# Two attention loops: TensorE's order written out by hand, with top-k and index scores rearranged

## The chip, the core and the metric
The kernel runs on one core of a Trainium2 chip. Its time is the device time of one execution in microseconds; several runs are taken and their median counts. One further execution was profiled by the hardware profiler. TensorE (PE in the profile; its weight loads are PEld), VectorE (DVE), ScalarE (ACT) and GpSimd (POOL) each run their own instructions in order and wait for one another by semaphores; SyncE's queue (SP) issues DMAs.

## The reference
Two blocks, one behind the other, on 512 tokens of width 1024; the change touches the second block, in which 16 meta tokens stand ahead of the tokens (528 positions). It has a differential attention (DA, 8 heads of two scores each), a feed-forward part, a sparse attention (DSA, 16 heads in 8 pairs) and a second feed-forward part. Cut to the core:

```python
# DA: two softmaxes a head, one subtracted from the other
s = einsum('bqhcd,bkhcd->bhcqk', q, k); p = softmax(where(causal, s, -inf))
o = einsum('bhqk,bkhe->bqhe', p[:, :, 0] - lam * p[:, :, 1], v)      # then rms norm per head, @ w_o
# DSA: an index decides which 128 keys a query sees (the 16 meta tokens always)
raw = einsum('bqhd,bkd->bqhk', qi, ki) * IDX_DIM ** -0.5             # 8 index heads, one index key
score = einsum('bqhk,bqh->bqk', relu(raw), wi)
score = where(causal & (k_pos < N_META), BIG_SCORE, score)
top_val, top_idx = top_k(where(causal, score, -inf), 128)
p = softmax(scores of the chosen keys); o = p @ v                    # @ w_o
```

## The kernel before
Everything is kept transposed: features on the 128 partitions, tokens along the free dimension. A float32 matrix product is made of three products: weights and inputs are split into a high part (written by ScalarE) and a low remainder (written by VectorE), and high x high, low x high and high x low are summed in one PSUM bank. A weight chunk of 128 x 1024 (512 KB) is loaded by SP into one of four buffers (`wload`), and split by `wchunk` into `wH` (L318, ScalarE) and `wL` (L320, VectorE), of which there are four each; `wget` keeps one chunk ahead. A projection of one head (`project`) is `gemm` (L349) on one chunk: two column cuts (272 and 256 columns), 24 products each (8 blocks of 128 rows times 3), then `rope` (L821): ScalarE copies the bank, VectorE shuffles, multiplies and adds, POOL multiplies (L827 to L831).

PSUM has eight banks, given out by tag: `g` 3 (projections), `s` 2 (scores), `t` 2 (transposes), `o` 1 (the output of a head). Scores read stacked copies of q and k: `stack` (L1034) writes high part and remainder of each half of the partitions (ScalarE and VectorE, four operations each for q and k), `swapped` (L1045) copies the halves crosswise with two DMAs (`k3`). These copies have one buffer, so the next head's are written behind the last scores of this one.

A head (DA) or pair (DSA) goes over four query blocks i of 128 with growing key ranges (144, 272, 400, 528). For each: S_i makes scores, masks them (L1227 in DA, L1422 in DSA, VectorE, with the row maximum), exponentials on ScalarE (L1234, L1429), and a scaling on VectorE (L1239 subtracts the second softmax, L1435 divides). T_i is one function: `turns_of` (L1139) transposes by TensorE (L1147) and copies the banks out (L1149 VectorE, L1151 ScalarE), and the value products (L1248, L1443 and L1448) follow. N finishes the head, X writes the stacked copies for the next head. F projects k of the next head, G projects q of the one after; in DA heads 0 and 2 G first makes a quarter of the values (`project_v`, L849). In the last heads F and G are early output products (`out_first`). The meta tokens' own attention (`metas`, with L1126 and L1135) runs in head 6, one step behind each of its steps. `attend` (L1353) calls these in the order of

```python
ORDER = "S1 S2 T1 F S3 T2 S4 X T3 T4 N G".split()
```

but this sets only priorities: a planner (the tile scheduler) puts every engine's instructions in order when the program is built, by dependencies, by priority and by the times it expects. So single products of F and G stand on TensorE between the attention steps, wherever the planner expected a hole. Only `front` (L493) fixes TensorE's order by `manual_schedule`.

DSA begins with `dsa_index` (L1483): the index key `ki` with its stacked forms `k2` and `k3` (made by three ScalarE and two VectorE operations, L1516 to L1522), and for each of four index head pairs a projection over 512 columns, `rope`, `stack` (`q2`, one buffer), and scores, relu on ScalarE (L1535) and a weighted sum into `sel` on VectorE (L1539, L1541). Then come the values (four quarters of five token tiles), then `dsa_topk` (L1543): 14 rounds over the four query blocks of a maximum of eight (L1557) and their replacement (L1558) on VectorE, and then q and k of pair 0 and q of pair 1.

Of the kernel before, what the change touches and what calls it, by code (L numbers as in the profile page):

```python
# [16 lines left out]
P = 128  # L17
D = 1024
KB = 8
# [14 lines left out]
ORDER = "S1 S2 T1 F S3 T2 S4 X T3 T4 N G".split()  # L34
# [178 lines left out]
class _Kernel:  # L213
# [135 lines left out]
    def gemm(self, w, H, L, cuts, M=P, spread=False, late=False):  # L349
# [4 lines left out]
        for c0, cn in cuts:  # L354
# [11 lines left out]
            yield ps[:M, :cn], c0, cn  # L366

# [771 lines left out]
    def turns_of(self, pool, srcs, name, width):  # L1139

        nc = self.nc
        t = pool.tile([P, width * P], F32, name=name)
        for c0 in range(0, len(srcs), 4):
            ps = self.ps("t")
            n = min(4, len(srcs) - c0)
            for j in range(n):
                nc.tensor.transpose(ps[:, P * j:P * j + P], srcs[c0 + j], self.ident)  # L1147
            if c0 == 4:
                nc.vector.tensor_copy(t[:, P * c0:P * (c0 + n)], ps[:, :P * n])  # L1149
            else:  # L1150
                nc.scalar.activation(t[:, P * c0:P * (c0 + n)], ps[:, :P * n], AF.Copy)  # L1151
        return [t[:, P * j:P * j + P] for j in range(len(srcs))]
# [10 lines left out]
    def da(self, g_next):  # L1163
        nc, T = self.nc, T2
        with ExitStack() as ctx:
# [38 lines left out]
            qk, scores, ps_, sums = {}, {}, {}, {}  # L1204

            def project(h, nm):

                t = self.acc if nm == "q" else self.rb
                self.rope(wp, self.gemm(self.wblocks(KB), self.hH, self.hL, self.cuts(T)), C, S, t)
                self.meta_keep(h, nm, t)  # L1210
                qk[nm] = t
# [4 lines left out]
            def soft(h, i):  # L1216

                t0, e = STARTS[i], ENDS[i]
                mx = self.sm.tile([P, 4], F32, name="mx2")
                p = ps_[i] = wp.tile([P, 2, T2], F32, name="p")  # L1220
                den = self.sm.tile([P, 4], F32, name="den2")
                m = 1 if i < 4 else 2
                for r in range(2):
                    for u, (pp, k0, k1) in enumerate(scores[h](i, r)):
# [4 lines left out]
                                                       accum_out=mx[:, c:c + 1])  # L1229
                if m == 2:  # L1230
                    nc.vector.tensor_tensor(mx[:, 0:2], mx[:, 0:4:2], mx[:, 1:4:2], ALU.max)
# [8 lines left out]

            def apply(h, i, po):

                a = ps_[i][:, 0]

                aT = self.turns_of(wp, [a[:, :P]] + [a[:, META + P * j:META + P * j + P] for j in range(i)], "aT", 5)
# [47 lines left out]
            def start(h, i, po):  # L1293
# [4 lines left out]
                soft(h, i)  # L1298
# [15 lines left out]
            def fill(h, op):  # L1314
                if op == "F":
                    if h < 7:
                        project(h + 1, "k")
                    else:
                        self.out_first(OH, OL, (2, 3, 4))
                else:  # L1320
                    if h in (0, 2):
                        self.project_v(vs, 2 + h // 2, self.vweights(), self.tok_tiles(T))
                    if h < 6:
                        project(h + 2, "q")
                    else:
                        self.out_first(OH, OL, (0, 1) if h == 6 else (5, 6, 7))

            project(0, "q")
            project(0, "k")
            stacks(0)  # L1330
            project(1, "q")
            self.attend({"S": start, "T": apply_flip, "N": finish, "X": stacks}, fill, metas)
# [5 lines left out]
    def out_first(self, H, L, ms, lo=0):  # L1338

        for m in ms:  # L1340
            for ps, c0, cn in self.gemm(self.wblocks(4), H[:4], L[:4], self.cuts(T2, lo)):
                x = self.x[m][:, c0:c0 + cn]
                self.nc.vector.tensor_tensor(x, ps, x, ALU.add)

# [8 lines left out]
    def attend(self, fns, fill, meta):  # L1353


        for h in range(8):
            po = self.ps("o")
            for op in ORDER:
                if op in ("F", "G"):
                    fill(h, op)  # L1360
                    if h == 6 and op == "F":
                        meta = meta()
                elif op == "X":
                    if h < 7:
                        fns["X"](h + 1)
                elif op[0] == "N":
                    fns["N"](h, po)
                else:
                    fns[op[0]](h, int(op[1]), po)
                    if h == 6 and not callable(meta):  # L1370
                        next(meta, None)

    def dsa(self, g_next):
# [3 lines left out]
        with ExitStack() as ctx:  # L1377
# [8 lines left out]
            with ExitStack() as ictx:  # L1386
                self.dsa_index(self.pool(ictx, "ei", 1, reuse_waits="tile"), C, S, sel)
                for q in range(4):
                    self.project_v(vs, q, self.vweights(), self.tok_tiles(T), meta=v0)
                self.dsa_topk(sel)  # L1390
# [5 lines left out]
            qk, scores, ps = {}, {}, {}  # L1396
# [5 lines left out]
            def project(b, nm):  # L1402
                t = self.acc if nm == "q" else self.rb
                cuts = self.cuts(T, lo if nm == "q" else 0)
                self.rope(wp, self.gemm(self.wblocks(KB), self.hH, self.hL, cuts), C, S, t)
                self.meta_keep(b, nm, t, lo)
                qk[nm] = t
# [4 lines left out]
            def soft(b, i, po):  # L1412
# [3 lines left out]
                mx = self.sm.tile([P, 4], F32, name="mx2")  # L1416
# [262 lines left out]
```

## Time and profile before

| | us |
|---|---|
| median of 3 runs (2151.54 to 2156.41) | 2152.59 |
| profiled execution | 2149.52 |
| its span, from the first to the last instruction | 2147.5 |

| busy in the span | PE | PEld | DVE | ACT | POOL |
|---|---|---|---|---|---|
| us | 2064.2 | 1885.1 | 1487.0 | 1023.3 | 277.8 |
| share | 96% | 88% | 69% | 48% | 13% |

The first block takes about the first 700 us, DA 700 to 996, the feed-forward part to 1393, DSA to about 1750 (index, values and top-k to 1527), the last feed-forward part the rest. Matmuls overlap in the pipeline and their ends are modelled, so a PE that is busy need not be at its peak; an instruction's duration is its way through the pipeline and not its distance to the next. Idle time of an engine is put down to what ended it. Window rows give busy time with the number of instructions; PEclk is the granted share of TensorE's clock.

### The profile page before, as it was taken

The numbers are of one execution on the slowest core, as the hardware profiler recorded it, in microseconds if no ns is written. First come the engines' busy times: TensorE is split into PE (matmuls) and PEld (weight loads), VectorE is DVE, ScalarE is ACT, GpSimd is POOL, SyncE is SP. The second block draws the span as 40 slices with busy tenths as digits, with TensorE's granted clock in tenths as the row PEclk, the third lists the DMA queues.
The fourth block names the chain that finished last, engine by engine and source line by source line (L and its number), as shares of the span: only waits on it lengthen the run. The fifth ranks groups of instructions, "written<-read, shape, count | busy, mean of one in ns | idle before, by whom it ended". The sixth has DMA issues, their size and how long they took to land.

```text
span 2147.5 us, 37629 instructions
## 1 busy us (share of the span) xinstructions
PE 2064.2 (96%) x14812; PEld 1885.1 (88%) x14812; DVE 1487.0 (69%) x3215; ACT 1023.3 (48%) x1874; POOL 277.8 (13%) x433
## 2 busy tenths in 40 slices
PE   8999999989998999889999999989899999999998
PEld 6788888877778888889999999979888899999997
DVE  7786777787776676866763566489888657735653
ACT  6876555346675455544442343353455444423431
POOL 0211111141103321212000000210211020000001
PEclk9999999999999999989999999999999999999998
DMA  5433342403212222212333333311322123332321
GB/s 192 123 117 115 96 125 94 143 25 108 68 60 70 80 72 68 71 50 80 92 95 90 90 89 89 99 50 50 100 60 76 55 73 95 89 99 89 99 81 48
DMA packets 59567, 186.11 MB, mean 87 GB/s; under 512 B 8384, under 2 KB 12480, under 8 KB 59392
## 3 DMA queue, kind: packets, MB, share of 16 engines
q1 hardware_dynamic: 58240, 182.68, 28.3%
q8 instruction: 116, 1.90, 0.4%
q10 hardware_dynamic: 1152, 1.05, 0.1%
q14 instruction: 59, 0.48, 0.1%
HBM read 171.77 MB, written 2.23 MB: 81 GB/s over the span
## 4 chain that ended last, share of the span: by engine, by line
PE 77%; DVE 11%; ACT 6%; issue 3%; POOL 1%; DMA 1%; SPq 0%; POOLq 0%; DVEq 0%; ACTq 0%
PE ps_g L364 48%; PE ps_s L364 14%; DVE wL L320 2%; PE ps_s L1062 2%; PE ps_o L1448 1%; PE ps_t L1147 1%; PE ps_g L849 1%; DVE sel L1558 1%; PE ps_o L1248 1%; DVE m L1557 1%; PE ps_s L766 1%; ACT wH L318 1%; PE ps_o L1001 1%; ACT q L1041 1%; PE ps_g L502 1%
## 5 line engine op out<-in xcount | busy, mean ns | idle before, releaser
L364 PE MATMUL ps_g<-hH,wL 128*128 128x256 f32 (+3 forms) x1856 | 590.4, 318 | 2.1 <-DVE wL L320 2.0
L364 PE MATMUL ps_g<-hH,wH 128*128 128x256 f32 (+3 forms) x1856 | 590.6, 318 | 0.0
L364 PE MATMUL ps_g<-hL,wH 128*128 128x256 f32 (+3 forms) x1856 | 590.3, 318 | 0.0
L318 ACT ACTIVATE wH<-raw 128x1024 fp32r<-128x1024 f32 x294 | 309.4, 1057 | 380.9 <-PE ps_g L364 203.3
L320 DVE TENSOR_TENSOR wL<-raw,wH 128x1024 fp32r<-128x1024 f32 x294 | 362.8, 1237 | 154.4 <-ACT wH L318 153.8
L364 PEld LDWEIGHTS ps_g<-hH,wL 128*128 128x128 f32 x1856 | 350.6, 189 | 26.0 <-DVE wL L320 3.5
L364 PEld LDWEIGHTS ps_g<-hL,wH 128*128 128x128 f32 x1856 | 350.4, 189 | 23.0 <-issue 2.9
L364 PEld LDWEIGHTS ps_g<-hH,wH 128*128 128x128 f32 x1856 | 350.4, 189 | 22.7 <-issue 1.0
L364 PE MATMUL ps_s<-hH,wH 128*128 128x256 f32 (+5 forms) x568 | 165.1, 291 | 6.6 <-ACT hH L393 6.6
L364 PE MATMUL ps_s<-hH,wL 128*128 128x256 f32 (+5 forms) x568 | 164.7, 290 | 0.0
L364 PE MATMUL ps_s<-hL,wH 128*128 128x256 f32 (+5 forms) x568 | 164.7, 290 | 0.0
L384 POOL TENSOR_TENSOR acc<-acc,sq 128x512 f32<-128x512 f32 (+3 forms) x62 | 78.7, 1269 | 545.1 <-ACT sq L383 543.8
L1600 DVE SCALAR_TENSOR_TENSOR c<-u,prm,c 128x528 f32<-128x528 f32 (+1 forms) x176 | 132.4, 755 | 1.5
L830 POOL TENSOR_TENSOR rt<-rt,S 128x272 f32<-128x272 f32 (+3 forms) x80 | 81.8, 1024 | 354.1 <-DVE rt L828 284.4
L364 PE MATMUL ps_g<-aH,wH 128*128 128x256 f32 (+1 forms) x418 | 118.7, 284 | 0.3 <-ACT aH L865 0.2
L364 PE MATMUL ps_g<-aL,wH 128*128 128x256 f32 (+1 forms) x418 | 118.7, 284 | 0.0
L364 PE MATMUL ps_g<-aH,wL 128*128 128x256 f32 (+1 forms) x418 | 118.6, 284 | 0.0
L364 PEld LDWEIGHTS ps_s<-hH,wH 128*128 128x128 f32 (+2 forms) x568 | 106.1, 187 | 8.3 <-ACT hH L393 6.6
L364 PEld LDWEIGHTS ps_s<-hH,wL 128*128 128x128 f32 (+2 forms) x568 | 106.3, 187 | 2.5 <-issue 1.0
L364 PEld LDWEIGHTS ps_s<-hL,wH 128*128 128x128 f32 (+2 forms) x568 | 106.1, 187 | 2.4 <-DVE hL L398 1.3
L1062 PE MATMUL ps_s<-k,q 128*128 128x272 f32 (+3 forms) x400 | 90.5, 321 | 12.9 <-DVE q L1042 4.3
L865 ACT ACTIVATE aH<-sg 128x528 fp32r<-128x528 f32 (+1 forms) x44 | 28.1, 639 | 124.3 <-DVE sg L1605 124.3
(551 smaller groups left out, 4586.1 us busy)
## 6 DMA issues: line engine op xcount, KB each, us to landing
raw<-in_ws_dram SPq DMA_DIRECT2D x294, 512.0 KB, 3.6
k<-k SPq DMA_DIRECT2D x32, 264.0 KB, 3.1
m<-acs_d SPq DMA_DIRECT2D x32, 256.0 KB, 3.5
e<-eas_d SPq DMA_DIRECT2D x32, 96.0 KB, 2.7
x<-in_xT_dram SPq DMA_DIRECT2D x8, 256.0 KB, 5.0
xo<-in_xT_dram SPq DMA_DIRECT2D x8, 256.0 KB, 5.6
k<-k SPq DMA_DIRECT2D x4, 256.0 KB, 6.5
out_dram<-x SPq DMA_DIRECT2D x8, 128.0 KB, 1.7
```

What stands on the lines that cost most here:

```text
L318: nc.scalar.activation(H, self.raw, AF.Copy)
L320: nc.vector.tensor_tensor(L, self.raw, H.bitcast(F32), ALU.subtract)
L364: nc.tensor.matmul(ps[:M, :cn], w[k][a][:, :M], b[k][:, c0:c0 + cn], start=i == 0, stop=i == 3 * n - 1)
L384: (eng or nc.gpsimd).tensor_tensor(acc, acc, s[:, :cn], ALU.add)
L502: mm(ps, w, h, start=k == 0 and a == 0, stop=False)
L766: nc.tensor.matmul(yd[64 * r:64 * r + 64, P * c:P * c + P], xdt[:, c, 2 * i + r, :], ms[2 * i + r][:, P * c:P * c + P], start=True, stop=True)
L830: nc.gpsimd.tensor_tensor(t, t, S[:, cc], ALU.mult)
L849: nc.tensor.matmul(ps[:tn, :256], a[k][:, t0:t0 + tn], w[k][b], start=n == 0, stop=n == 3 * KB - 1)
L865: nc.scalar.activation(H[:, cols], src, AF.Copy)
L1001: nc.tensor.matmul(po[64 * r:64 * r + 64, P * j:P * j + w], vs[j][:, 64 * kv:64 * kv + 64], pT[r][:, 256 * j:256 * j + w], start=j == 0, s ...
L1062: nc.tensor.matmul(ps, q[:, r, t0:e], k[:, r, k0:k1], start=n == 0, stop=n == 1)
L1600: nc.vector.scalar_tensor_tensor(c[:, lo:], u[:, t + lo:t + T2], self.col(fw, 3 * b + t), c[:, lo:], ALU.mult, ALU.add)
```

## The change
TensorE's order in both loops is now as written: `attend` runs inside `manual_schedule` for TensorE, with a longer ORDER. In it f and g stand for portions of F and G: a projection is four portions of 12 products (two for each cut, `portions`), and what F or G has is dealt evenly over the f's or g's that are left. T is now the transposes alone (up to two banks of four), U a third bank, V the value products, Z4 the second score of block 4 (S4 is the first). M runs a step of the meta tokens' attention, now M4 and M5 of head 6 and M1 to M3 of head 7. The early output products become half jobs of one cut (12 products): in head 6 four in G, in head 7 four in F and eight in G, the second cuts ahead of the first, and each pair of output blocks keeps its weights between. Other engines' order is still the planner's.

In DSA, `dsa_index` makes q of two index pairs ahead (two buffers for `q2`), puts two quarters of the values ahead of the scores of pairs 2 and 3, and swaps k2 into k3 by two DMAs. `dsa_topk` goes block by block; the first block, of 128 keys, looks for the 16 lowest on the negated and mirrored scores (2 rounds) in place of the 112 highest (14 rounds).

```diff
-ORDER = "S1 S2 T1 F S3 T2 S4 X T3 T4 N G".split()
+ORDER = "S1 f S2 M1 f T1 M2 S3 V1 f M3 T2 S4 V2 f Z4 T3 X g V3 M4 g g T4 g U4 V4 M5 N".split()
...
+    def portions(self, w, H, L, c0, cn, then, n=2):
...
+        def part(i):
+            if not ps:
+                ps.append(self.ps("g")[:, :cn])
+            ww = w()
+            steps = [(k, a, b) for k in range(len(H)) for a, b in ((0, H), (1, H), (0, L))]
+            m = len(steps)
+            for j in range(m * i // n, m * (i + 1) // n):
+                k, a, b = steps[j]
+                self.nc.tensor.matmul(ps[0], ww[k][a], b[k][:, c0:c0 + cn], start=j == 0, stop=j == m - 1)
+            if i == n - 1:
+                then(ps[0])
+        return [lambda i=i: part(i) for i in range(n)]
...
+        cs = list(range(0, len(srcs), 4))
+        banks(cs[:2])
+        return [t[:, P * j:P * j + P] for j in range(len(srcs))], lambda: banks(cs[2:])
...
+    def out_fill(self, H, L, h, op, lo=0):
+        if h == 6:
+            jobs = [(m, 1) for m in range(4)]
+        elif op == "F":
+            jobs = [(m, 1) for m in range(4, 8)]
+        else:
+            jobs = [(m, 0) for m in range(8)]
+        return [lambda j=j: self.out_first(H, L, [j], lo) for j in jobs]
...
+        with self.tc.manual_schedule(engines={mybir.EngineType.PE}):
+            for h in range(8):
+                po = self.ps("o")
+                todo = {op: fill(h, op.upper()) for op in "fg"}
+                for n, op in enumerate(ORDER):
+                    i = int(op[1]) if len(op) > 1 else 0
+                    if op in todo:
+                        left = ORDER[n:].count(op)
+                        for f in range(-(-len(todo[op]) // left)):
+                            todo[op].pop(0)()
+                    elif op[0] == "M":
+                        if (h, i) in ((6, 4), (6, 5), (7, 1), (7, 2), (7, 3)):
+                            next(meta, None)
...
+            self.dsa_topk(wp, sel)
+            for f in project(0, "q") + project(0, "k"):
+                f()
             stacks(0)
+            for f in project(1, "q"):
+                f()
...
-        nc.scalar.activation(k3[64:], ki[64:], AF.Copy)
-        nc.vector.tensor_tensor(k3[:64], ki[64:], k3[64:].bitcast(F32), ALU.subtract)
+        k3 = self.swapped(ip, k2, "k3")
...
+            q2[b] = self.stack(ip, q, "q2", META, 2)
...
+        project(0)
+        project(1)
+        for b in range(4):
+            if b < 2:
+                scores(b)
+                project(b + 2)
+            else:
+                values(b - 2)
+                scores(b)
+        values(2)
+        values(3)
...
-        for rnd in range((TOPK - META) // 8):
-            for i in range(1, 5):
-                m8 = self.sm.tile([P, 8], F32, name=f"m8{i}")
-                rest = sel[i][:, META:]
+            rest = neg if i == 1 else sel[i][:, META:]
+            if i == 1:
+                nc.vector.tensor_scalar(neg[:, ::-1], diag, -1.0, None, ALU.mult)
+            for rnd in range(2 if i == 1 else (TOPK - META) // 8):
+                m8 = self.sm.tile([P, 8], F32, name="m8")
                 nc.vector.max(m8, rest)
                 nc.vector.match_replace(rest, m8, rest, MARK)
```

## Rows read from the trace of the kernel before

**Rows 1.** Busy time by stretch, one row each: start and end, length, engines.
```profile
core 0: us, PE busy (x) PEld busy (x) DVE busy (x) ACT busy (x) POOL busy (x), PEclk, DMA share, GB/s
867.00:890.70 23.70, 21.09 (x162) 19.73 (x162) 19.92 (x70) 14.36 (x41) 6.04 (x12) 1.00 0.25 70
1573.10:1597.00 23.90, 23.53 (x190) 20.83 (x190) 20.37 (x67) 13.54 (x33) 4.00 (x7) 1.00 0.25 68
985.00:1392.00 407.00, 406.71 (x3336) 405.67 (x3334) 238.30 (x354) 150.45 (x184) 25.61 (x65) 1.00 0.31 91
914.50:971.80 57.30, 51.35 (x375) 48.28 (x376) 37.44 (x135) 25.64 (x76) 7.70 (x13) 0.88 0.17 48
1668.60:1725.10 56.50, 52.69 (x410) 46.46 (x411) 37.36 (x137) 24.66 (x66) 1.96 (x3) 0.94 0.17 48
1505.00:1527.30 22.30, 17.25 (x126) 16.48 (x124) 17.54 (x36) 8.32 (x14) 10.37 (x16) 0.92 0.48 143
```

**Rows 2.** Groups of TensorE's instructions in one DA head: busy, mean ns, idle before.
```profile
L1248 PE MATMUL ps_o<-v,aT 128*128 128x128 f32 x28 | 4.2, 290 | 0.6 <-ACT aT L1151 0.5
L1147 PE MATMUL ps_t<-ident,p 128*128 128x128 f32 x14 | 2.2, 276 | 2.0 <-DVE p L1239 2.0
```

**Rows 3.** Chain of work in the feed-forward stage: start, us, what.
```profile
1016.85 3.02 PE ps_g L364 x24
1019.88 2.83 PE ps_s L364 x24
```

**Rows 4.** Timeline of a DA head from S1 to T1: start, us, instruction, idle.
```profile
884.84 0.43 PE L1062 MATMUL ps_s<-k,q 128*128 128x144 f32 x2
...
886.35 0.30 DVE L1227 CUSTOM_DVE_ANT_0 p<-ps_s,wide 128x144 f32<-128x144 f32 x1
...
886.80 1.22 DVE L320 TENSOR_TENSOR wL<-raw,wH 128x1024 fp32r<-128x1024 f32 x1
...
890.97 0.41 PE L1147 MATMUL ps_t<-ident,p 128*128 128x128 f32 x2 [1.15 <-DVE p L1239]
```

**Rows 5.** The page's DMA issues, the swapped copy: count, size, us to landing.
```profile
k<-k SPq DMA_DIRECT2D x32, 264.0 KB, 3.1
```

**Rows 6.** Timeline of TensorE in DA's head 6, products of the meta tokens.
```profile
926.67 1.48 PE L1135 MATMUL ps_t<-mv,v 128*128 128x16 f32 x8 [1.82 <-DVE mv L1264]
```

**Rows 7.** Timeline of TensorE, first scores of head 0, in DA and DSA.
```profile
742.08 0.43 PE L1062 MATMUL ps_s<-k,q 128*128 128x144 f32 x2
...
746.73 0.45 PE L1062 MATMUL ps_s<-k,q 128*128 128x144 f32 x2 [1.03 <-DMA k<-k]
...
1520.74 0.33 PE L1062 MATMUL ps_s<-k,q 128*128 128x144 f32 x1 [2.86 <-DVE k L1042]
...
1527.34 0.42 PE L1062 MATMUL ps_s<-k,q 128*128 128x144 f32 x2 [0.92 <-DMA k<-k]
```

**Rows 8.** Timeline of TensorE in a DSA head: value products, then projection products.
```profile
1577.73 0.44 PE L1448 MATMUL ps_o<-pT,v 128*64 128x128 f32 x4
1578.10 0.38 PE L364 MATMUL ps_g<-hH,wL 128*128 128x256 f32 x1
1578.32 0.28 PE L364 MATMUL ps_g<-hL,wH 128*128 128x256 f32 x1
```

**Rows 9.** Top-k on VectorE: the chain, then the timeline of blocks 1 and 2.
```profile
1477.79 1.19 DVE sel L1558 x2
...
1481.20 1.19 DVE sel L1558 x2
...
1497.10 0.61 DVE L1557 MAX8 m<-sel 128x8 f32<-128x128 f32 x2
...
1497.69 0.27 DVE L1558 MATCH_REPLACE8 sel<-m,sel 128x128 f32<-128x128 f32 x1
```

**Rows 10.** Timeline of TensorE in the index: first scores of pairs 0 and 1.
```profile
1417.50 0.45 PE L1062 MATMUL ps_s<-k,q 128*128 128x144 f32 x2 [2.35 <-DVE q L1042]
...
1427.17 0.45 PE L1062 MATMUL ps_s<-k,q 128*128 128x144 f32 x2 [0.93 <-DVE q L1042]
```

More of the change, by code (lines that the diff above doesn't have):

```diff
@@ L1229, in soft @@
                                                        accum_out=mx[:, c:c + 1])
+                if 1 not in rs:
+                    return
                 if m == 2:
@@ L1336, in da, with out_first @@
             self.out_last(OH, OL, g_next)
-    def out_first(self, H, L, ms, lo=0):
-        for m in ms:
-            for ps, c0, cn in self.gemm(self.wblocks(4), H[:4], L[:4], self.cuts(T2, lo)):
+    def out_first(self, H, L, jobs, lo=0):
+        for m, half in jobs:
+            if m not in self.wo:
+                self.wo[m] = self.wblocks(4)
+            for ps, c0, cn in self.gemm(self.wo[m], H[:4], L[:4], self.cuts(T2, lo, half)):
                 x = self.x[m][:, c0:c0 + cn]
                 self.nc.vector.tensor_tensor(x, ps, x, ALU.add)
+    def out_fill(self, H, L, h, op, lo=0):
[6 more added lines that the diff above has]
+        return [lambda j=j: self.out_first(H, L, [j], lo) for j in jobs]
     def out_last(self, H, L, g_next, lo=0):
@@ L1353, in attend @@
     def attend(self, fns, fill, meta):
[L1356 to L1371, printed above, removed]
+        self.wo = {}
+        with self.tc.manual_schedule(engines={mybir.EngineType.PE}):
[11 more added lines that the diff above has]
+                            next(meta, None)
+                    elif op == "X":
+                        if h < 7:
+                            fns["X"](h + 1)
+                    elif op == "N":
+                        fns["N"](h, po)
+                    elif op[0] in "SZ":
+                        fns["S"](h, i, (0, 1) if i < 4 else (0,) if op[0] == "S" else (1,))
+                    elif op[0] == "V":
+                        fns["V"](h, i, po)
+                    else:
+                        fns[op[0]](h, i)
     def dsa(self, g_next):
@@ L1386, in dsa @@
             with ExitStack() as ictx:
[L1387 to L1390, printed above, removed]
+                values = lambda q: self.project_v(vs, q, self.vweights(), self.tok_tiles(T), meta=v0)
+                self.dsa_index(self.pool(ictx, "ei", 1, reuse_waits="tile"), C, S, sel, values)
             oc = self.pool(ctx, "eo", 1, reuse_waits="tile")
```

183 lines of the change are left out of this document (104 added, 79 removed).

## The prediction
> **What bounds the kernel now.** I read the busy times by stretch first. In the feed-forward stage TensorE is full: weight loads busy 405.67 of 407.00 us, matmuls back to back. In one steady head of the first attention (DA) weight loads are busy 19.73 of 23.70 us, VectorE 19.92; in one of the sparse attention (DSA) 20.83 of 23.90, VectorE 20.37 [rows 1]. So both loops have gaps on TensorE, and VectorE stands close behind: whatever closes the gaps, a head can't go much under 20 us. Next the groups of TensorE instructions of the DA head, for who ended the gaps: 2.0 us are transposes that wait for the softmax (DVE p), 0.6 us value products that wait for the copied transposes [rows 2]. Then the chain, for the price of dense work: 24 products of 272 columns take 3.02 us, of 256 columns 2.83 [rows 3]; so a portion of 12 is 1.51 or 1.42 us. The timelines come last, for single waits.
>
> **DA, a steady head.** Removed: the order in which the scheduler strews projection products between attention steps. A head has six such waits (2.6 us of idle), and each also shows the tail of a product, 0.28 long where the next could start after 0.12, so 6 x 0.16 = 1.0: 3.6 us in all. Added: fixed places, where every later TensorE instruction stands behind a late one. The first transposes (T1) stand behind a portion, S2 and a portion: 1.5 + 0.5 + 1.5 = 3.5 us after S1. In the trace S1 ends at 885.27 and T1 starts at 890.97, 5.7 us later, because VectorE first finished a rope and did a weight split of 1.22 us between links of the chain [rows 4]. VectorE's order is still the scheduler's, so this wait lies between 0 and 2.2 us; I take 1.0, nearer to the middle since of the 5.7 us the split (1.22) and the queue before the first score operation (1.08) are not the chain's own. T4 stands 5.9 us behind the last scores, with eight stacking operations of ScalarE and VectorE for the next head between: 0 to 1.5, I take 0.5. T2, T3 and the four value steps: 0.7 (now 0.6 by rows 2). Step X (stacks, then two DMAs of 3.1 us [rows 5] for the swapped copy) starts behind Z4 as now behind S4, for it needs the buffers; it has 9.4 us of TensorE work until the next S1 and needs about four splits and a DMA: 0.3. New waits 2.5, old 3.6: -1.1 us a head; ends -3.3 (only the value steps wait) and +2.4 (6.0 of waits). Four heads without value projections: -4.4. Heads 0 and 2 have 14 us more TensorE work (5 token tiles of 24 products) and the same softmax, so VectorE has room and its waits go: -2.5 each, -5.0. DVE, ScalarE, POOL and DMA operations stay the same in number; weight loads follow their portions, in the same order on SP's queue, and a load of 512 KB is four buffers ahead.
>
> **DA, both ends.** In head 6 no projection is left: of the last two heads' 57.30 us weight loads are busy 48.28, at a granted clock of 0.88 [rows 1], and the products of the meta tokens alone waited 1.82 us for VectorE [rows 6]. The change cuts the early output projections into 16 half jobs (1.42 to 1.51 us) and lays 4 of them and the meta steps between the steps of head 6. Its 28.4 us should come to 23.5: -4.9; head 7, with work for 27.4 in its 28.9: -1.5. All four weight chunks of the half jobs now stay in the four buffers until the second halves ran, so the next stage's first split can start only behind two of the eight jobs in head 7; six jobs (8.5 us) cover its 2.3 us, and it would cost those 2.3 if they didn't. At the start S1 of head 0 waits for the DMA of the swapped keys; now 25 products ran in that hole (742.3 to 746.7) and TensorE idled only 1.03 us [rows 7]. Fixed, they come behind S1: 25 x 0.12 = +3.0. DA in all: -4.4 - 5.0 - 4.9 - 1.5 + 3.0 = **-12.8** (ends -28 and +6).
>
> **DSA, the loop.** Idle is small, but the strewn order costs at each change of kind: a projection product behind four value products has its successor 0.22 us later [rows 8] instead of 0.12; with the way in I put an estimated 0.25 on one block. The head's timeline has twelve such blocks of transposes or value products among projections (one is shown), the new order nine: -0.75; waits for copied transposes are 0.3 idle with tails 0.75. Of these 1.5 I leave 0.5 for new waits: -1.0 us a head, six heads -6.0; ends -1.5 and +2.4 as in DA. Splitting S4 by head (S4, Z4) costs nothing: its four score products need the same two banks now, and a portion between lets VectorE empty them. U4 needs a bank that ScalarE empties in one copy, under the portion g. Heads 6 and 7 took 56.50 us at a clock of 0.94 [rows 1]; two heads at 22.9, 5.8 of extra output products and 1.5 of meta steps are 53.1: -3.4. Sum **-9.4** (ends -16 and +14).
> Weighed against a rule: the DSA head shows matmuls busy 23.53 of 23.90 us but weight loads 20.83 [rows 1]. The Trainium skill (Perfetto Trace Analysis, Identifying the Most-Contended Engine) holds matmul busy share a poor measure of headroom and weight-load share a good one. By the first the loop has 0.4 us a head to give, by the second 3.1, so six heads would give 2 or 19 instead of 6; the feed-forward row, with 405.67 of 407.00, agrees with the second, but the blocks that stay keep their price, and I stay with 1.0.
>
> **DSA, the front.** Top-k is 14 rounds of four query blocks at 3.41 us [rows 9], VectorE full all along. The first block now takes 2 rounds on the flipped sign (112 of up to 128 keys: the same choice by its complement). Its part of a round is half of the two maxima and their overlap, 0.22, and 0.25 of replacing [rows 9]: 12 x 0.47 = 5.6, less 0.4 for the two flips: -5.2. Order by block instead of by round makes each operation wait for the one before: where nothing else fills, 84 operations lose the overlap of about 0.08, +6.7; where blocks 3 and 4 or the ropes fill, 0. I take 0 as the scheduler already pairs blocks here. k3 by two DMAs in place of two ScalarE and one VectorE operation: -0.7 on VectorE; the DMA (3.1) lands while S1 still waits for q2. These waits are 2.35 us for the first q2 and 0.93 for the second, which had to wait for the only buffer [rows 10]: a second buffer takes -1.5 with the tails; the values placed between change nothing, they fill there now. After top-k 22.30 us pass until the swapped keys are there, VectorE busy 17.54 [rows 1, 7]: weight splits and ropes that stood behind top-k. In the dependent gaps of the last block some can go earlier; 0 to 8 us, I take 4. And S1 waits for the keys without filler: 26 products ran in that hole [rows 7], +3.1. The sum is -5.2 - 0.7 - 1.5 - 4.0 + 3.1 = **-8.3** (ends -15 and +4).
>
> **Sum.** -12.8 - 9.4 - 8.3 = -30.5 us against the profiled execution's 2149.52, so 2119.0; the median of the runs stands 3.07 above it: **2122**.
>
> **Rivals.** (a) *Other engines set the period*: softmax, ropes and stacks on VectorE (19.9 to 20.4 us a head and in order) hold the steady heads where they are; then only the front, the ends and the heads with values pay: -8.3 - 4.9 - 1.5 + 3.0 - 3.4 and -2 for values, -17: 2135. For it: VectorE's 84% in steady heads; against it: it idles 3.8 us there, waiting for TensorE in turn.
> (b) *The fixed order stalls*: a late softmax holds TensorE's whole queue, projections too, that now run in its place. Price: T1's full 2.2 us, T4's 1.5 and the rest 2.3, 6.0 a head; minus 3.6 it is +2.4 in DA and, with 1.5 saved less, +2.4 at most in DSA. Over 12 steady heads +29, with the ends and the front -15: 2167, slower. It decides from the point where the new waits pass 4.9 us a head in DA (3.6 + 15/12). For it: the 5.7 us of rows 4; against it: the own chain of T1 is some 3 us.
> (c) *TensorE goes dense*: hardly a new wait; DA -28, DSA loop -12, front -13: 2100.
> (d) *Top-k in order by block loses what its shorter first block gives*: the front gives 0, the rest stays: 2130.
> That the loops don't do what the change says, I can rule out: the order is written out.
>
> **How the numbers follow.** Forecast with (d) beside it 0.55, (a) 0.2, (c) 0.15, (b) 0.1. About 0.2% (4.3 us) is what a measurement of this kernel can tell from no change. Faster by more: all but (b) and a tail of (a) that comes down to nothing, 0.83; within: that tail, 0.07; slower: 0.10. The range from 2098, the ends of (c), to 2150, the tail of (a), leaves out most of (b) and what is under (c).
>
> **What would show it.** Right: steady heads of 22 to 23 us in both loops, with transposes idle under 2 us a head; head 6 of DA under 25 us at full clock; S1 of DSA's head 0 some 8 us earlier behind the index; in the loops runs of 12 products between steps. Wrong: T1 or T4 idle over 2 us a head, S1 waiting for the swapped keys in steady heads, or top-k as long as before. The biggest doubt is VectorE's order, which the change leaves to the scheduler and the trace of before can't show.

## The result, and the profile after

The changed kernel is slower: 2185.73 us median (2184.26 to 2189.62) against 2153.73 us for the kernel before on the same chip, a ratio of 1.0152 [1.0137, 1.0167]. The forecast was 2122 us and the range ended at 2150; rival (b), the fixed order that stalls, had been given 0.10 and 2167. The profiled execution of after is the one of 2189.62 us, 40 us above that of before. To find these 40 us I cut both traces at four marks: the first scores of DA, the first product of the feed-forward stage behind it, VectorE's first instruction on DSA's index keys, and DSA's first scores. The loops of all runs below are read by the same cuts; a loop here ends with the first product of the next feed-forward stage.

| us between marks | DA loop | DSA front | DSA loop |
|---|---|---|---|
| before | 254.4 | 125.3 | 232.0 |
| after | 275.0 | 129.2 | 246.1 |
| forecast | 241.6 | 117.0 | 222.6 |

All three stages went the other way; the other stages differ by 2 us together. The busy times by stretch answer rows 1 (same columns): a steady DA head, a steady DSA head, then the last head of each loop, of the changed kernel.

```profile
core 0: us, PE busy (x) PEld busy (x) DVE busy (x) ACT busy (x) POOL busy (x), PEclk, DMA share, GB/s
...
881.30:908.40 27.10, 21.11 (x164) 19.60 (x163) 21.06 (x70) 14.35 (x40) 6.09 (x12) 1.00 0.22 59
1608.60:1634.50 25.90, 22.60 (x191) 20.23 (x190) 20.45 (x67) 13.29 (x33) 3.82 (x8) 1.00 0.22 63
...
961.40:995.10 33.70, 32.75 (x239) 32.04 (x238) 21.90 (x78) 14.56 (x42) 2.70 (x6) 0.90 0.19 55
1737.30:1770.40 33.10, 31.50 (x256) 29.59 (x256) 21.02 (x74) 12.84 (x35) 0.00 (x0) 0.95 0.19 57
```

A DA head takes 27.10 us where it took 23.70, a DSA head 25.90 where it took 23.90. TensorE is not busier (weight loads 19.60 against 19.73), nor is any other engine near full: both sides wait for each other. TensorE's groups in that DA head answer rows 2:

```profile
L1082 PE MATMUL ps_s<-k,q 128*128 128x272 f32 (+3 forms) x21 | 4.6, 321 | 1.6 <-DVE mx L1266 1.3 <-DMA k<-k 0.2
L1294 PE MATMUL ps_o<-v,aT 128*128 128x128 f32 x28 | 4.0, 282 | 2.6 <-ACT aT L1173 2.6
L1169 PE MATMUL ps_t<-ident,p 128*128 128x128 f32 x14 | 2.2, 276 | 1.8 <-DVE p L1280 1.8
```

Idle is now 1.6 + 2.6 + 1.8 = 6.0 us against 2.6: the 3.4 us by which the head grew. The transposes wait about as long as before (1.8 against 2.0); new are the value products, which wait 2.6 for ScalarE's copy of the transposes, and the scores, 1.6. What ScalarE does meanwhile is in its timeline (start, us, instruction, idle before):

```profile
888.19 0.63 ACT L1275 ACTIVATE p<-p,mx 128x400 f32<-128x400 f32 x1 [1.56 <-DVE mx L1273]
888.72 0.19 ACT L1275 ACTIVATION_READ_ACCUMULATOR p<-p,mx 128x1 f32 x1
888.82 0.61 ACT L1275 ACTIVATE p<-p,mx 128x400 f32<-128x400 f32 x1
...
889.43 0.47 ACT L1173 ACTIVATE aT<-ps_t 128x384 f32<-128x384 f32 x1
```

and in TensorE's:

```profile
887.39 0.49 PE L1169 MATMUL ps_t<-ident,p 128*128 128x128 f32 x3
887.64 0.79 PE L1082 MATMUL ps_s<-k,q 128*128 128x272 f32 x4
889.95 0.94 PE L1294 MATMUL ps_o<-v,aT 128*128 128x128 f32 x6 [1.52 <-ACT aT L1173]
```

The transposes of T2 are done near 887.9, yet their copy starts at 889.43: ScalarE works in order, and the exponentials of block 3 stand ahead of the copy and themselves waited 1.56 us for VectorE. Between T2 and V2 the order has only S4 (0.8 us) as cover. In the kernel before, with scores and transposes next to each other, the same copy ran ahead of those exponentials:

```profile
872.84 0.48 ACT L1151 ACTIVATE aT<-ps_t 128x384 f32<-128x384 f32 x1
...
874.20 0.63 ACT L1234 ACTIVATE p<-p,mx 128x400 f32<-128x400 f32 x1 [0.31 <-DVE mx L1232]
```

The late end of the head shows VectorE's order, ahead of T4:

```profile
894.94 1.21 DVE L322 TENSOR_TENSOR wL<-raw,wH 128x1024 fp32r<-128x1024 f32 x1
...
896.60 1.40 DVE L1062 TENSOR_TENSOR q<-acc,q 64x512 fp32r<-64x512 f32 x2
898.03 0.70 DVE L1062 TENSOR_TENSOR k<-rb,k 64x528 fp32r<-64x528 f32 x1
...
899.49 0.77 DVE L1280 SCALAR_TENSOR_TENSOR p<-p,den 128x528 f32<-128x528 f32 x1
...
900.40 0.74 PE L1169 MATMUL ps_t<-ident,p 128*128 128x128 f32 x5 [1.45 <-DVE p L1280]
```

One weight split and three of the four stacks for the next head lie in the softmax of the last block, and T4 waits 1.45 us for it. Last, the first scores of both loops (rows 7):

```profile
743.03 0.23 PE L1082 MATMUL ps_s<-k,q 128*128 128x144 f32 x1
748.41 0.91 PE L1082 MATMUL ps_s<-k,q 128*128 128x144 f32 x3 [5.15 <-DMA k<-k]
...
1547.03 0.49 PE L1082 MATMUL ps_s<-k,q 128*128 128x144 f32 x1 [8.49 <-DVE k L1062]
1551.42 0.89 PE L1082 MATMUL ps_s<-k,q 128*128 128x144 f32 x3 [3.91 <-DMA k<-k]
```

Without filler S1 waits 5.15 us in DA (1.03 before). In DSA it waits 8.49 us for the split of the keys on VectorE, because top-k, 1447.5 to 1502.8 us before, now runs from 1497.3 to 1563.7, past the loop's start.

### The profile page after: what moved, and what is told of

Same layout as the page of the kernel before. It is cut to its first block, busy times and chain, and to the rows that moved or that the text cites. A ratio compares the mean times of both kernels' runs of the same rounds, so it can differ in the third digit from the quotient of the medians.

```text
span 2187.9 us, 37566 instructions
## 1 busy us (share of the span) xinstructions
PE 2057.7 (94%) x14812; PEld 1884.6 (86%) x14812; DVE 1490.6 (68%) x3179; ACT 1019.2 (47%) x1872; POOL 269.7 (12%) x433
## 4 chain that ended last, share of the span: by engine, by line
PE 71%; DVE 17%; ACT 5%; issue 5%; POOL 2%; DMA 1%; SPq 0%; POOLq 0%; DVEq 0%; ACTq 0%
PE ps_g L366 41%; PE ps_s L366 14%; PE ps_g L382 3%; PE ps_g L869 3%; DVE wL L322 2%; PE ps_s L1082 1%; DVE rt L848 1%; DVE q L1062 1%; DVE sel L1663 1%; DVE m L1662 1%; PE ps_s L786 1%; DVE k L1062 1%; DVE p L1505 1%; POOL rs_r L433 1%; PE ps_g L522 1%
## 5 line engine op out<-in xcount | busy, mean ns | idle before, releaser
L366 PE MATMUL ps_g<-hH,wL 128*128 128x512 f32 (+3 forms) x1344 | 443.5, 330 | 1.3 <-DVE wL L322 1.1
L366 PE MATMUL ps_g<-hL,wH 128*128 128x512 f32 (+3 forms) x1344 | 442.2, 329 | 0.0
L366 PE MATMUL ps_g<-hH,wH 128*128 128x512 f32 (+3 forms) x1344 | 442.0, 329 | 0.0
L366 PEld LDWEIGHTS ps_g<-hH,wL 128*128 128x128 f32 x1344 | 253.4, 189 | 23.7 <-DVE wL L322 2.4
L366 PEld LDWEIGHTS ps_g<-hH,wH 128*128 128x128 f32 x1344 | 253.3, 188 | 22.8 <-issue 1.0
L366 PEld LDWEIGHTS ps_g<-hL,wH 128*128 128x128 f32 x1344 | 253.5, 189 | 21.0 <-issue 1.0
L382 PE MATMUL ps_g<-hH,wH 128*128 128x256 f32 (+2 forms) x512 | 152.5, 298 | 0.0
L382 PE MATMUL ps_g<-hL,wH 128*128 128x256 f32 (+2 forms) x512 | 146.1, 285 | 0.0
L382 PE MATMUL ps_g<-hH,wL 128*128 128x256 f32 (+2 forms) x512 | 145.8, 285 | 0.0
L1082 PE MATMUL ps_s<-k,q 128*128 128x272 f32 (+3 forms) x400 | 84.8, 325 | 40.2 <-DMA k<-k 11.4
```

Of the source, the lines that this page charges most:

```text
L366: nc.tensor.matmul(ps[:M, :cn], w[k][a][:, :M], b[k][:, c0:c0 + cn], start=i == 0, stop=i == 3 * n - 1)
L382: self.nc.tensor.matmul(ps[0], ww[k][a], b[k][:, c0:c0 + cn], start=j == 0, stop=j == m - 1)
L1082: nc.tensor.matmul(ps, q[:, r, t0:e], k[:, r, k0:k1], start=n == 0, stop=n == 1)
```

## The experiments

Each ratio below is to the kernel before on the same chip; three chips were used, on which that kernel took 2151.92 to 2154.24 us, so times of two experiments can differ by some 2 us for that alone. Three theories follow: the written order stalls at single places that lack cover (the copies first); VectorE's own order behind it; and, in the front, top-k that starts late and lengthens. Rivals: the cutting costs by itself, or the period is another engine's and each wait only moves.

**The order, left to the scheduler (e1).** In `attend`:

```
-        with self.tc.manual_schedule(engines={mybir.EngineType.PE}):
+        if True:
```

> The changed kernel, but TensorE's order inside the two attention loops is left to the scheduler again; portions, separate steps, half jobs and the new front stay. Theory F (the fixed order itself stalls TensorE): the steady heads come back from 27.1 to about 23.7 us in DA and from 25.9 to about 23.9 in DSA, the start of each loop gets its filler back; of the 20.6 us lost in DA and 14.1 lost in and behind the DSA loop some 30 return, while the front keeps its +3.9: about 2155 us (2148 to 2163). Rival G (the cutting into portions, steps and half jobs costs by itself, whoever orders it): steady heads stay over 25.5 us and the time over 2172.

Measured: 2156.91 us, 1.0013 [1.0003, 1.0023]: 29 of the 32 us that the change cost are back. DA 257.8, front 129.9, DSA loop 234.3 us. Theory F holds; the front keeps its loss. The steady heads are a partial miss: DSA's came to 24.3 us, DA's only to 25.5 to 25.8, not 23.7 (below, the kernel with the sequence of before shows why). A DA head:

```profile
875.30:900.80 25.50, 21.64 (x165) 20.62 (x164) 20.15 (x70) 13.91 (x39) 6.11 (x12) 0.96 0.23 61
```

**The value steps one portion later (e3).** One edit of the order, in both loops:

```
-... S3 V1 f M3 T2 S4 V2 f Z4 ...
+... S3 f V1 M3 T2 S4 f V2 Z4 ...
```

> The changed kernel with one edit of the fixed order: the value steps V1 and V2 stand one portion of 12 products later (f V1, f V2 in place of V1 f, V2 f). Theory C (V1 and V2 wait because the copy of the transposes stands on ScalarE behind the exponentials of the next block, and only one score step of TensorE covers it): the waits of V1 and V2 fall from 2.9 us a head in DA and 1.6 in DSA to under 1 and 0.5; nearly all of it comes back: some 2 us a head in DA, 1 in DSA, about 2162 us (2155 to 2170). Rival P (VectorE's and ScalarE's chain sets the period, and the wait moves to the next step, T2 or S2): heads change by under 0.5 us, 2178 to 2188.

Measured: 2163.88 us, 1.0051 [1.0033, 1.0068], 22 us less than after. DA 267.6 (7.4 less), front 128.7, DSA loop 228.3 (17.8 less). Busy times of a DA and a DSA head, and TensorE's groups with a wait in that DA head:

```profile
906.70:932.90 26.20, 22.13 (x164) 21.18 (x164) 20.28 (x70) 14.27 (x40) 6.74 (x12) 0.93 0.22 62
1620.30:1643.40 23.10, 22.18 (x189) 20.28 (x188) 20.16 (x67) 13.51 (x33) 3.85 (x8) 1.00 0.25 70
```
```profile
L1294 PE MATMUL ps_o<-v,aT 128*128 128x128 f32 x28 | 4.7, 319 | 0.0
L1082 PE MATMUL ps_s<-k,q 128*128 128x272 f32 (+3 forms) x21 | 4.4, 319 | 0.9 <-DVE mx L1266 0.9
L1169 PE MATMUL ps_t<-ident,p 128*128 128x128 f32 x14 | 2.3, 280 | 3.1 <-DVE p L1280 2.9 <-DVE mx L1273 0.3
```

The wait for the copy is gone, 2.6 to 0.0. In DSA all of it is gained and more: 23.10 us is below the 23.90 of before, so head for head a fixed order can beat the scheduler's there. In DA theory P is half right: idle falls only from 6.0 to 4.0, since the transposes' wait grows from 1.8 to 3.1, and a part of the gain is lost to the clock, 0.93 in this head (the heads on both sides of it take 27.4 and 27.0 us from first scores to first scores).

**Banks for S2 (e6).** In `pair_scores`, on top of the last kernel:

```
+        return lambda i, r: self.scores(q2, ks, i, r, "g" if i == 2 else "s")
...
```

> As e3_v_later, but the scores of the second query block (S2) of both loops go into banks of the projections' three in place of the scores' two. Theory B (S2 waits because the two banks of S1 are not yet emptied by VectorE, one portion after S1): the waits of scores for VectorE's masking, 12.2 us over DA and 2.8 over DSA, fall to under 5, and 6 to 10 us come back: 2154 to 2158. Rival: VectorE is late anyhow, so the wait moves to the first transposes, or to a portion that finds no bank: 2161 to 2167.

Measured: 2167.70 us, 1.0077 [1.0062, 1.0093]. TensorE's group of transposes in one DA head, and that head's busy times:

```profile
L1169 PE MATMUL ps_t<-ident,p 128*128 128x128 f32 x14 | 2.4, 293 | 4.4 <-DVE p L1280 4.4
```
```profile
907.50:935.20 27.70, 23.12 (x162) 22.62 (x162) 20.14 (x70) 14.18 (x40) 6.73 (x12) 0.88 0.21 58
```

The scores wait no more, the transposes 1.3 us longer: the rival is right. S2's wait for a bank was no price of its own but the first place at which TensorE met a late VectorE.

**Less work on VectorE (e10).** On top of the value steps moved, inside the loops; this kernel leaves the low parts of the weights out of the sums, with all products in place:

```
-        nc.vector.tensor_tensor(L, self.raw, H.bitcast(F32), ALU.subtract)
+        nc.gpsimd.memset(L.bitcast(F32), 0.0)
...
```

> As e3_v_later, but inside the two loops the low parts of the weights aren't computed on VectorE (1.22 us each, two a head): GpSimd writes zeros in their place, so the products with the low parts add nothing; all TensorE work stays. Theory W (T4 of DA waits 2.6 us because VectorE, in its own order, does four stack operations and a weight split between the links of the last block's softmax): T4's wait falls by about the split's 1.2 us, the slow-clock spell behind it goes, and the DA heads come from 26.2 to 24 to 25 us; DSA, where T4 hardly waits, stays near 23: 2148 to 2155. Rival (the exponentials on ScalarE, or the scores' own time, set T4): DA heads stay over 25.8 us, 2160 to 2166.

Measured: 2145.96 us, 0.9968 [0.9958, 0.9977]. A DA and a DSA head:

```profile
873.90:898.50 24.60, 20.65 (x164) 19.67 (x164) 19.04 (x68) 14.27 (x40) 8.78 (x14) 1.00 0.23 66
1606.60:1628.90 22.30, 22.30 (x189) 20.53 (x189) 18.61 (x65) 13.66 (x33) 5.61 (x10) 1.00 0.27 72
```

DSA's heads come down by 0.8 us. DA's heads 3 to 5, from first scores to first scores 27.4, 26.2 and 27.0 us, take 24.5 each and have the full clock; T4's wait fell from 2.4 to 1.6. Theory W holds for that wait, and the total is a little under what it expected. But TensorE's idle in these DA heads fell only from between 4.1 and 4.9 us to between 3.9 and 4.0, since earlier transposes of the head now wait 1.0: most of what they gained is the clock. So the whole gain (18 us) is no price for the splits alone; the keys of each DSA head come earlier too.

**T4 with more cover (e9).** The last value products and the head's end go behind the next head's first scores, on top of the value steps moved; the front is the mended one of below (values behind the index scores, top-k in rounds):

```
-S1 f S2 M1 f T1 ... M4 g g T4 g U4 V4 M5 N
+S1 f U4' V4' N' S2 M1 f T1 ... M4 g g g M5 T4      (': of the head before)
```

> The front of e8_mix, and in both loops a fixed order in which the last block's value products and the head's end stand behind the next head's first scores and a portion, so that T4 comes a portion later and S2 too. Theory L (the fixed order loses only where a step has too little TensorE work ahead of it): the waits of T4 (2.6 us a head in DA in e3) and of S2 for VectorE (1.1) fall under 1 us together; steady heads 23 to 24 us in DA at full clock and 22.5 to 23 in DSA, against 26.2 and 23.1: 2122 to 2134. Rival: S1 has 1.1 us less of work ahead of it since the stacks, and waits for the swapped keys by as much as T4 gains: DA heads over 25 us, 2140 to 2150.

Measured: 2141.39 us, 0.9955 [0.9940, 0.9969]. Against e3 the DA loop is 7.4 us shorter (260.2, still 5.8 over before), the front 7.4 and the DSA loop 6.1. DSA heads take 22.6 us as expected. DA's take 24.5 to 25.2: the scores' wait fell to 0.6, but a whole portion more (1.4 us) ahead of T4 left its wait at 2.0 to 2.1 us (2.4 before the move). Both the expectation and its rival missed: S1 had no wait for the keys in the head from 876.8, the softmax of the last block just ended later too. So in DA T4's wait follows VectorE, whose order the scheduler makes for the sequence that it is given.

**The front: values behind the index scores (e2).**

```
         for b in range(4):
+            scores(b)
             if b < 2:
-                scores(b)
                 project(b + 2)
-            else:
-                values(b - 2)
-                scores(b)
-        values(2)
-        values(3)
+        for q in range(4):
+            values(q)
```

> The changed kernel with the four value projections of DSA all behind the index scores again, as before the change; top-k by block, the two query buffers and the loops stay. Theory V (values between the index scores delay the start of top-k by two quarters, some 36 us, and its end then holds the first scores of the loop): top-k starts near 1460 instead of 1497 and ends before the loop's first score; the 8.7 us that TensorE waits there for the split of the keys go, with the slow clock behind it, and the 2.8 us wait of the first transposes; the scores of the index wait a little more for their queries and for ScalarE (up to 4 us): 10 to 14 us gained, 2172 to 2176. Rival: the front is TensorE's work in any order, and the unfilled waits of the index take back what the end of top-k gives: 2181 to 2187.

Measured: 2181.28 us, 1.0131 [1.0116, 1.0146], 4 us less, the smaller of the two answers. Top-k does start 24 us earlier against the front's start (55.5 us behind it, not 79.5), but still takes 60.7 us, so S1 waits 6.5 us for the split keys and 5.8 for the swapped ones. The front fell by 1.1 us only, the DSA loop by 4.2.

**Both edits at once (e4).** The scheduler's order and the values behind:

> Both edits: the loops' order left to the scheduler, and the values of DSA behind the index scores. If the loops' loss is the fixed order's and the front's loss that of the late top-k, the two add up: the front, with a top-k of 44 instead of 56 pairs of operations, gains 3 to 6 us on the kernel before, and the loops equal it: 2146 to 2152, level with the kernel before or just below. If the cutting costs by itself: over 2160.

Measured: 2144.97 us, 0.9958 [0.9941, 0.9974], just under the expected span (DA 257.8, front 128.1, DSA 223.8). The two do more than add up: together they gain 40.8 us on the changed kernel, alone 28.8 and 4.5. The rest is in the DSA loop, 10.5 us shorter than with the free order alone, where top-k ran into its start.

**Top-k in rounds (e5)**, on top of both:

```
-            for rnd in range(2 if i == 1 else (TOPK - META) // 8):
+        for rnd in range((TOPK - META) // 8):
+            for i in range(1, 5):
+                if i == 1 and rnd > 1:
+                    continue
...
```

> As e4_free_values_back, but top-k again in rounds over the query blocks (the first block in the first two rounds only), 44 pairs of operations as in the change. Theory D (by block, each operation waits for the one before on the same rows; e4 takes 60.8 us for 44 pairs, 1.38 each, the kernel before 55.3 for 56, 0.99 each): top-k takes 43 to 47 us, the 6.7 us that TensorE waits for the split keys ahead of the loop shrink to under 2, and the front from 128.1 to 121 to 123: 2138 to 2141 us. Rival: what lies between the operations on VectorE (ropes, weight splits) makes the length, not their order: top-k stays over 56 us and the time at 2143 to 2147.

Measured: 2136.81 us, 0.9933 [0.9916, 0.9949]: 8 us less, 5.4 by the ratios. Replacements of blocks 2 to 4 (count, ns min/median/max, first and last start) in the changed kernel, in the kernel with both edits, and in rounds:

```profile
L1663 DVE MATCH_REPLACE8 sel<-m,sel x42: 407/542/687, 1498.8 to 1564.2; 128x256 f32<-128x256 f32 x14, 128x384 f32<-128x384 f32 x14, 128x512 f32<-128x512 f32 x14
```
```profile
L1660 DVE MATCH_REPLACE8 sel<-m,sel x42: 408/543/681, 1457.0 to 1516.6; 128x256 f32<-128x256 f32 x14, 128x384 f32<-128x384 f32 x14, 128x512 f32<-128x512 f32 x14
```
```profile
L1663 DVE MATCH_REPLACE8 sel<-m,sel x42: 409/550/692, 1453.2 to 1501.2; 128x256 f32<-128x256 f32 x14, 128x384 f32<-128x384 f32 x14, 128x512 f32<-128x512 f32 x14
```

The operations last the same (542 to 550 ns), the stretch is 65.4, 59.6 and 48.0 us. Theory D holds, though top-k takes 49.2 us and not 43 to 47. From the first maximum to the end of the last, by block and in rounds:

```profile
1455.40:1516.20 60.80, 60.80 (x521) 59.40 (x520) 58.45 (x144) 19.01 (x33) 1.46 (x5) 1.00 0.21 63
1451.50:1500.70 49.20, 49.20 (x422) 47.64 (x421) 49.14 (x140) 15.89 (x31) 1.23 (x4) 1.00 0.17 55
```

VectorE is busy 58.45 of 60.80 us by block and 49.14 of 49.20 in rounds; the durations of its instructions within these stretches sum to 61.8 and 58.4, so neighbours overlap for 3.3 and 9.3 us. Order by block so costs 2.3 of idle and 6.0 of lost overlap, 8.3 of the 11.6; the rest is more work, above all three weight splits (8 instead of 5, 1.2 us each) that stood between.

**The mended versions.** First (e8) DA with the step sequence of before and a free scheduler, DSA with the moved value steps, front mended:

```
+DA_ORDER = "S1 M1 S2 M2 T1 V1 M3 f f f f S3 T2 V2 S4 Z4 X T3 V3 M4 T4 U4 V4 M5 N g g g g".split()   # free
+DSA_ORDER = "S1 f S2 M1 f T1 M2 S3 f V1 M3 T2 S4 f V2 Z4 T3 X g V3 M4 g g T4 g U4 V4 M5 N".split()   # fixed
...
```

> The new front with values behind the index scores and top-k in rounds; DA with the order of the kernel before and the scheduler free (portions and half jobs stay cut); DSA with the fixed order of e3_v_later. If the fixed order gains in DSA once the value steps have cover (steady heads 23.1 us in e3 against 23.9 before) and the cutting costs nothing in DA: DA 254 us as before, front 122, DSA loop up to the feed-forward stage 220 to 223: 2131 to 2137. If the cutting itself costs DA the 3.4 us that it lost in e1 and e4 (257.8 us): 2136 to 2141.

Measured: 2129.97 us, 0.9895 [0.9879, 0.9911]. Steady DA heads are back at 23.7 us with the portions still cut, so in DA neither the cutting nor the free scheduler but the written sequence cost 2 us a head (e1 has it free too, at 25.5); fixing it cost some 1.5 more (27.1). DA takes 246.7 us, 7.7 less than before; the gain is in heads 6 and 7, where half jobs and the steps of the meta tokens now stand between the others (which of the two gave it was not tried). A steady DA head, then heads 6 and 7:

```profile
871.70:895.40 23.70, 21.13 (x162) 19.76 (x162) 19.89 (x70) 14.34 (x40) 6.02 (x12) 1.00 0.25 67
919.20:964.90 45.70, 44.78 (x365) 42.41 (x366) 34.56 (x134) 25.24 (x76) 6.16 (x13) 1.00 0.13 38
```

The two heads take 45.7 us at clock 1.00, against 57.30 at 0.88 [rows 1] (1.3 us of it went to the stretch behind the loop's last head, and the loop's start is 2.6 longer). With the sequence of before in DSA as well, and free (e12):

> As e8_mix, but DSA too has the order of the kernel before and the scheduler free: what stays of the change is the cutting into portions and half jobs, and the mended front. It prices the fixed order in DSA alone: if that was worth the difference of steady heads (23.1 against 23.9 us before), DSA's loop becomes 4 to 6 us longer than in e8, 2133 to 2137; if the gain of e8 in DSA came from the half jobs at the ends, the time stays at 2128 to 2132.

Measured: 2131.71 us, 0.9909 [0.9892, 0.9925]; DSA loop 224.0 against 222.8 us. The heads are 23.9 us as expected and cost 3.5 us in all (five, cut at their last value products), but the loop's end, where its half jobs fall behind the last head, is 1.6 shorter and its start 0.7: the fixed order of the moved value steps is worth 1.2 us in DSA, a difference the two ratios don't tell apart. With the order of T4' in DSA and two portions ahead of S1 in head 0 (e11):

```
+                if order is not DA_ORDER and h == 0:
+                    todo["f"].pop(0)()
+                    todo["f"].pop(0)()
...
```

> As e8_mix, but DSA takes the fixed order of e9_next_head, and its head 0 runs two portions of the next keys ahead of its first scores. If a fixed order pays where each step has cover: DSA heads 22.6 us instead of 23.1, the 2.0 to 5.7 us wait for the swapped keys at the loop's start partly filled: 2122 to 2127. If the start is only moved (the portions delay the keys' own rope and stack on VectorE): 2127 to 2131.

Measured: 2125.98 us, 0.9882 [0.9865, 0.9899], the lowest of all medians, though its interval and e8's overlap. Steady DSA heads take 22.6 us; S1's wait at the loop's start is 3.0 us. Cutting at that S1, front and DSA loop are 126.6 and 215.2, together 341.8, against 344.0 in e8. A steady DSA head:

```profile
1613.40:1636.00 22.60, 22.07 (x191) 20.19 (x190) 20.03 (x67) 13.53 (x34) 4.07 (x7) 1.00 0.25 73
```

## Why the prediction was wrong

**The steady heads: wrong, and the step is the sum of the new waits.** For a DA head I had put 2.5 us against 3.6 removed, and the point from which rival (b) decides at 4.9. By the idle of the groups the new head has 6.0, the old 2.6. Term by term:

| wait, us a DA head | put | bounds | measured |
|---|---|---|---|
| T1 (measured: with T2, T3) | 1.0 | 0 to 2.2 | 0.35 |
| T4 | 0.5 | 0 to 1.5 | 1.45 |
| V1 to V4 (put: with T2, T3) | 0.7 | none | 2.6 |
| S1 for the swapped keys | 0.3 | none | 0.2 (0.8 in the head before) |
| scores for VectorE | none | none | 1.3 |

T1, the wait I bounded with most care, was fine. The value steps failed: I had priced them by rows 2, where the copy's wait is 0.6. But there T2's copy stood ahead of block 3's exponentials, and T1's, which stood behind those of block 2, could start as soon as its transposes were done:

```profile
867.01 0.51 ACT L1234 ACTIVATE p<-p,mx 128x272 f32<-128x272 f32 x1
...
867.71 0.38 ACT L1151 ACTIVATE aT<-ps_t 128x256 f32<-128x256 f32 x1
```

The new order puts a portion between a block's scores and the transposes of the block before. In ScalarE's order the exponentials now stand ahead of the copy, and when VectorE is late with their maximum the copy waits too, though its transposes are done; S3 or S4 alone is its cover. I followed VectorE's queue and not ScalarE's. The value steps' wait is the largest of the five, and moving two of the steps gave 22 us. The scores had no term at all; taking their banks away as a cause showed that their wait is VectorE's lateness, as is T4's. The saving failed too: of its 3.6 us the 2.6 of old waits gave way to 6.0 of new ones, and the 1.0 of tails didn't come, for the new head has six waits again and takes 21.1 us without its idle, like the old one.

**The heads with values: wrong.** Heads 0 and 2 were put at -2.5 each, because VectorE would have room there. Up to the last value product of head 3 (892 products of TensorE before, 886 after) the rows are:

```profile
742.10:863.00 120.90, 113.63 (x892) 106.11 (x891) 86.83 (x284) 65.98 (x169) 29.20 (x58) 1.00 0.29 79
743.00:876.30 133.30, 112.21 (x886) 106.53 (x885) 87.35 (x279) 65.64 (x169) 25.33 (x56) 0.97 0.26 72
```

That is +12.4 us where start and heads together were forecast at -4.2. TensorE idles 21.1 us in place of 7.3; in head 2 the two value steps alone wait 1.09 and 1.52, as in a steady head, since its values come in the g's behind them.

**DA beyond that.** The remaining loss is a mutual wait of TensorE and VectorE, which I had named as the biggest doubt. That VectorE's work ahead of the last link matters is shown for T4 (two splits of 1.2 us a head taken off: its wait 0.8 shorter); the heads then gained mostly by the clock. More cover on TensorE alone hardly shortens T4's wait (one portion later: 2.0 to 2.1), though the heads came down to 24.5 to 25.2 with it. Not tried is a VectorE order written for this TensorE order, so whether DA could gain from a fixed order stays open. Whether the 3.6 a head put on the strewn order can be had in DA at all is not shown: the fastest steady DA heads, 23.7, are strewn too.

**DA, both ends.** The mechanism was right, half jobs in heads 6 and 7 at full clock, and shows in e8: DA 7.7 us shorter. In after it is lost among the fixed order's waits: head 6 took 25.8 us instead of 23.5, head 7, with the twelve other half jobs now all ahead of its end, 33.7, and the stretch behind it to the feed-forward stage fell only from 24.7 to 22.9; together the three are 82.4 us against 82.0. The start was forecast at +3.0; the wait at S1 grew by 4.1.

**DSA, the loop.** Forecast -9.4, after +14.1. Here the same terms failed, as TensorE's groups of the head from 1608.60 show:

```profile
L1082 PE MATMUL ps_s<-k,q 128*128 128x272 f32 (+3 forms) x23 | 4.3, 309 | 0.9 <-DVE mx L1505 0.9
...
L1532 PE MATMUL ps_o<-pT,v0b 128*128 128x128 f32 x8 | 1.7, 300 | 1.2 <-ACT pT L1173 1.2
```

and the start took over the front's delay. Cut at the last value products, the start is 6.7 us longer, the five heads behind it 10.3, and the end 2.8 shorter. With the value steps moved and the front mended the loop is 222.8, -9.2, nearly the forecast: the steady heads gave 0.8 each where 1.0 was put, and the rest came mostly at the loop's end. That is the forecast's mechanism, but in an order that the change doesn't have. The rule of the Trainium skill (Perfetto Trace Analysis, Identifying the Most-Contended Engine) weighed there: from matmul busy time the head had 0.4 us to give, from weight loads 3.1. The fastest version's heads take 22.6 us, 1.3 less than before, so here the trace agrees with the rule that matmul busy time hides room; 1.8 of the 3.1 by weight loads were not had.

**DSA, the front: wrong at two steps.** "The values placed between change nothing" failed: they delay the last scores, and so top-k, by 24 us; its end fell on the loop's first scores. And order by block was taken at 0 out of 0 to 6.7; with the values behind it cost 8.3 (2.3 idle and 6.0 overlap), above the upper end. Rival (d) named it; that its price is 8.3 too is luck, for it was the whole credit of the front. The credit of 4.0 for splits in top-k's gaps was no gain: with the values behind three more did run there (8 instead of 5), and each lengthened top-k; in the changed kernel 5 ran there, as before, and top-k took 66.4 us with ropes, stacks and masks of the loop's start in it. In rounds top-k takes 49.2 us instead of 55.3, with the shorter first block, and the front, with its other edits, 121.9, -3.4.

**The chances.** Rival (b) had the right mechanism, with "the own chain of T1 is some 3 us" held against it; the chain that counted was another. Its price of +2.4 for a steady head was near (2.0 in DSA, 3.4 in DA); its sum was too low above all because it kept the gains of the front (-8.3, measured +3.9) and of DA's last heads (-6.4, measured +0.4). My forecast of 2122 is nearly reached by e11 at 2126, by orders that the change doesn't have.

## What to carry to other kernels

When steps are laid out by hand on one engine, list for every step the last thing that it waits for and the queue of the engine that makes it, and give it as much work ahead as that queue holds; the cheap step behind a copy is the one forgotten. A scheduler's order is fixed too when the program is built: "fixed" against "free" is one sequence against another, so compare sequences. Where one engine's order is written by hand and the others' is not, test a step's cover by moving it once before trusting the sum. Serial operations are to be interleaved over independent rows, and what starts a long serial stretch on another engine goes first, however well its filler fits.

## What the runs showed of the hardware

The clock often fell behind one long wait, as it did at all twelve waits of 2.73 to 2.78 us in DA's heads 2 and 4 to 6 of e1, e4 and e5. In the kernel with the value steps moved, T4 waits 2.39 us; a microsecond later the products stand 0.21 us apart instead of 0.12, the lower of the clock's two levels, and ten value products take 2.17 us:

```profile
924.22 0.74 PE L1169 MATMUL ps_t<-ident,p 128*128 128x128 f32 x5 [2.39 <-DVE p L1280]
...
925.15 0.28 PE L382 MATMUL ps_g<-hH,wH 128*128 128x256 f32 x1
...
925.83 0.41 PE L382 MATMUL ps_g<-hH,wL 128*128 128x256 f32 x1
926.05 0.41 PE L382 MATMUL ps_g<-hL,wH 128*128 128x256 f32 x1
...
926.90 2.17 PE L1294 MATMUL ps_o<-v,aT 128*128 128x128 f32 x10
```

That head's mean clock is 0.93; 0.07 of 26.20 us is 1.8, my estimate of what that cost. The changed kernel's head, with 6.0 us of idle in pieces of some 1.5 at most, kept 1.00. The length of a single wait does not decide it: in e2, whose DA loop is the changed one, the clock fell once at 789.5 us, behind waits of 0.83 and 0.93, and in e6 a wait of 2.79 us that ended at 818.7 left it at 1.00. So a repaired wait paid less than its length where the remaining one grew. I had not priced a wait by what it does to the clock behind it.
